# Expert values of a dense mixture, with the values as the stationary operand: 512-column matmuls become 256-column ones, and the closing transposes go

## The chip, the cores and the metric

The kernel is written in Bass and Tile for one core of a Trainium2 chip. The metric is the device time of one execution in microseconds (us). Five engines run side by side: TensorE (PE) multiplies matrices, VectorE (DVE) and ScalarE (ACT) work on vectors, GpSimd (POOL) and SyncE (SP) mostly issue transfers. A matmul multiplies a stationary operand of 128 x 128, which PE loads ahead of it (a weight load, PEld in the rows), with a moving operand of up to 512 columns, and adds into an accumulator in PSUM. PSUM has eight banks of 512 fp32 columns on each of 128 partitions.

## What is computed

The reference is one inference step of a two-layer hybrid decoder: a prompt of 256 tokens and 8 decode tokens, model width 1024. Each layer has four mixers, a cross-attention, and at the end an expert channel mixer over 16384 experts, of which every token picks 16 for each of 8 heads:

```python
act = jax.nn.gelu(jnp.einsum('td,thkd->thk', hb, u_tab[e]).astype(jnp.float32))
return jnp.einsum('thk,thkd->td', (g * act).astype(hb.dtype), v_tab[e])
...
x = x + peer_ffn(rmsnorm(x, lp['norm_ffn']), lp['peer_wq'], lp['peer_subkeys'], lp['peer_u'], lp['peer_v']).astype(x.dtype)
```

`u_tab` and `v_tab` have a row of 1024 for every expert. After the second layer a last rmsnorm gives the output.

## The kernel before

The kernel keeps the residual `x` with features in partitions: `x` is 128 partitions x 8 chunks x 264 tokens (256 prompt tokens, then 8 decode tokens), so feature f stands in chunk f // 128.

For the prompt tokens the experts are computed densely. Both tables are walked in 128 tiles of 128 experts x 1024 features (512 KB each). The first stage (`u_tile`, "u stage" below) multiplies each tile of `u_tab` with the normed tokens, 24 matmuls of 256 columns for each tile, and leaves in `HG0` and `HG1` the product of gate and gelu for every expert and token: experts of a tile in partitions, 256 tokens in columns, zero where a token has not picked the expert. The second stage ("value stage") multiplies these gates with `v_tab`. The 8 decode tokens go another way (`sample_u`, `sample_v`, `sample_out`).

Numbers are fp32, and products are made in three fp32r matmuls each: an operand is split in a high part (an ACT cast) and a low part (a DVE subtraction), and high x high, high x low and low x high are added. `load_w` does it for a weight tile (`w` is what the DMA brought, three buffers; `wh`, `wl` the parts, two buffers each), `split` for the gates (`ghl`, two buffers, tag `ga`). Every matmul is recorded at line 288, the line of the helper `mm`, so rows are told apart by the tiles that they name: `mm` for projections and the u stage, `pv` for the value stage, `var` for the sum of squares of the next rmsnorm, `tp` for transposes.

In the value stage of the kernel before the gates are stationary (128 experts x 128 tokens) and half a tile of values moves (512 features). Four accumulators `pv0` to `pv3` of 128 tokens x 512 features, one PSUM bank each, collect all 128 tiles: 2 halves of the tokens x 2 halves of the features x 3 products, 12 matmuls of 512 columns for a tile. At the end `total` takes each accumulator: ACT copies it out with the scale 1/GS (`ov`), PE transposes it in four pieces (`tp`), DVE adds them to `x`, ACT squares the sum, and PE adds the squares over the features with a matmul against a constant matrix (`var`).

The order of the instructions on each engine is set by the scheduler of the framework, save inside `tc.manual_schedule`, where PE keeps the order of the code. The tiles are loaded on SP's queue. In the middle of the value stage of the first layer (tile 62) `following()` starts the loads and small preparations of the next layer. After the value stage, in the first layer the next layer's input projection reads `x` through `eh` and `el` (scaled and split, ACT and DVE); in the second layer the last rmsnorm reads it (`yfin`, `rstd`).

Of the kernel before, what the change touches and what calls it, by code (L numbers as in the profile page):

```python
# [8 lines left out]
DEPTH, D, SEQ, DB = 2, 1024, 256, 8  # L9
NT = SEQ + DB  # L10
# [222 lines left out]
GS = 16384.0  # L233
# [10 lines left out]
def emit(tc, A, O, layers=(0, 1)):  # L244
    nc = tc.nc
    V, S, G, T = nc.vector, nc.scalar, nc.gpsimd, nc.tensor
# [8 lines left out]
    def load_consts(pool, grp):  # L255
        names = CGRP[grp]
        n = sum(coff[k][1] for k in names)
        t = pool.tile([128, n], F32, name="cst_" + grp)
        out, o, i = {}, 0, 0
        while i < len(names):  # L260
            j, s, w = i, coff[names[i]][0], 0
            while j < len(names) and coff[names[j]][0] == s + w:
                out[names[j]] = t[:, o + w:o + w + coff[names[j]][1]]
                w += coff[names[j]][1]
                j += 1
            nc.sync.dma_start(t[:, o:o + w], A['cst'][:, s:s + w])
# [20 lines left out]
    def mm(out, lhsT, rhs, start=True, stop=True, skip=False):  # L287
        T.matmul(out, lhsT, rhs, start=start, stop=stop, skip_group_check=skip)  # L288
# [8 lines left out]
    def tt(out, a, b, op, eng=None):  # L297
        (eng or V).tensor_tensor(out, a, b, op=op)  # L298
# [7 lines left out]
    def stt(out, a, s, b, op0, op1, **kw):  # L306
        V.scalar_tensor_tensor(out, a, s, b, op0=op0, op1=op1, **kw)

    def act(out, a, f, **kw):
        S.activation(out, a, f, **kw)  # L310

    def split(h, l, x):
        S.copy(h, x)  # L313
        tt(l, x, h.bitcast(F32), OP.subtract)

    x = gp.tile([128, 8, NT], F32, name="x")
    for c in range(0, 8, 2):
# [39 lines left out]
    def var(cols=NT):  # L357
        return ps([128, cols], "var", "pa")
# [109 lines left out]
    def layer(l, mx, v, following):  # L468
# [1126 lines left out]
    def peer(l, vc, xo, oo, xe, following):  # L1595
# [12 lines left out]
        fp = pe.enter_context(tc.tile_pool(name="f%d" % l, bufs=1, side="right", reuse_waits="tile"))  # L1608
# [14 lines left out]
        tp = te.enter_context(tc.tile_pool(name="t%d" % l, bufs=1, side="right", reuse_waits="tile"))  # L1623
        r = rstd(tp, v)
        hf = tp.tile([128, 8, NT], F32, name="hf", tag="sq")
        q = tp.tile([128, 16, NT], F32, name="pq")
        for c in range(16):
            if c == 4:
                rms(tp, vc('norm_ffn'), r, hf, (hh, hl))
                for j in range(2):  # L1630
                    o = ps([8, 512], "h8")
# [5 lines left out]
            o = proj(A['peer_wq'][l, c], eh if c < 8 else (hh, hl), tag="pr" if c in (2, 3, 4) else "mm")  # L1637
# [23 lines left out]
        for i in range(2):  # L1661
            s16 = tp.tile([128, 8, 2, 16], F32, name="s16")
            i16 = tp.tile([128, 8, 2, 16], U32, name="x16")
            for g4 in range(4):
                o = ps([128, 4, 128], "sc")
                for k in range(4):
                    c = g4 * 4 + k
# [7 lines left out]
            o = ps([128, 3, 128], "tp")  # L1675
# [12 lines left out]
        for c_ in range(2):  # L1688
# [17 lines left out]
        o = ps([128, 3, 8], "ex")  # L1706
# [48 lines left out]
        for t4 in range(64):  # L1755
            tsl = slice(t4 * 4, t4 * 4 + 4)
            a = fp.tile([128, 2, 2, 128, 2], F16, name="ga", bufs=2)
            b = fp.tile([128, 2, 2, 128, 2], F16, name="gb", bufs=2)
# [4 lines left out]
            o = ps([128, 4, 128], "g")  # L1763
# [5 lines left out]
            ov = o.rearrange("p t i -> p i t")  # L1769
# [8 lines left out]


        cur_tag[0] = "ps"  # L1780
        acc = [ps([128, 512], "pv%d" % i, ("pa", "pr")[i // 2]) for i in range(4)]
        nx = None
        for i2 in range(0, 128, 2):
            part = []
            for i in (i2, i2 + 1):
                vh, vl = (t.rearrange("p a b -> p (a b)") for t in load_w(A['vd'][l, i]))
                hs = HG0[:, i, :] if i < 64 else HG1[:, i - 64, :]
                ghl = fp.tile([128, 2, 256], F32R, name="ghl", tag="ga", bufs=2)
                split(ghl[:, 0], ghl[:, 1], hs)
                part.append((vh, vl, ghl[:, 0], ghl[:, 1]))  # L1790
            def terms(i, n):
                vh, vl, gh, gl = part[n]
                m, d = slice((i % 2) * 128, (i % 2) * 128 + 128), slice((i // 2) * 512, (i // 2) * 512 + 512)
                for k, (a, b) in enumerate(((gh, vh), (gh, vl), (gl, vh))):
                    mm(acc[i], a[:, m], b[:, d], start=i2 + n == 0 and k == 0, stop=i2 + n == 127 and k == 2)
            for n in range(2 if i2 < 126 else 1):
                for i in range(4):
                    terms(i, n)
            if i2 == 62:
                he.close()  # L1800
                nx = following()
            if i2 == 116:
                v = ps([128, NT], "var", "ps")
                s2 = fp.tile([128, 8, 8], F32, name="s2", tag="ua", bufs=2)
                act(s2, x[:, :, 256:264], AF.Square)
                act(warm, part[0][2][:, 0:1].bitcast(F32), AF.Sqrt, scale=0.0)
                for c in range(8):
                    mm(v[:, 256:264], cg['o1024'], s2[:, c, :], start=c == 0, stop=False, skip=True)


        def total(i):
            ov = fp.tile([128, 512], F32, name="ov", tag="gb", bufs=2)
            act(ov, acc[i], AF.Copy, scale=1.0 / GS)
            o = ps([128, 4, 128], "tp", "mm")
            for c in range(4):
                T.transpose(o[:, c, :], ov[:, c * 128:c * 128 + 128], ident)
            n = slice((i % 2) * 128, (i % 2) * 128 + 128)
            d = x[:, 4 * (i // 2):4 * (i // 2) + 4, n]
            tt(d, d, o, OP.add)
            s2 = fp.tile([128, 4, 128], F32, name="s2", tag="ga", bufs=2)  # L1820
            act(s2, d, AF.Square)
            return s2, n
        q = []
        with tc.manual_schedule(engines={mybir.EngineType.PE}):
            terms(0, 1)
            for i, nx_ in ((0, 2), (2, 1), (1, 3), (3, None)):
                if nx_ is not None:
                    terms(nx_, 1)
                q.append(total(i))
        for i, (s2, n) in enumerate(q):  # L1830
            for c in range(4):
                mm(v[:, n], cg['o1024'], s2[:, c, :], start=False, stop=i == 3 and c == 3, skip=True)
        cur_tag[0] = "pa"
        pe.close()
        return nx, v
# [9 lines left out]
    v = var()  # L1845
# [8 lines left out]
    for i, l in enumerate(layers):  # L1854
        nx, v = layer(l, nx, v, (lambda n=layers[i + 1]: Mix(n)) if i + 1 < len(layers) else last)
# [24 lines left out]
```

## Time and profile before

| | |
|---|---|
| median of 3 runs | 2437.68 us (2434.05 to 2437.69) |
| the profiled execution's own time | 2419.86 us |
| its span, first to last instruction | 2418.1 us |
| busy shares | PE 97%, PEld 88%, DVE 72%, ACT 57%, POOL 11% |
| value stage, first layer | 853.08 to 1206.05 us, 352.97 us |
| value stage, second layer | 2053.50 to 2404.72 us, 351.22 us |

The profile is one execution, 17.82 us below the median of the runs. A busy PE is not PE at its peak: a matmul's row lasts until its result is written, and rows overlap, so what a matmul costs in a stream is the spacing of the starts, and not the mean length of a row.

### The profile page before, as it was taken

What the parts mean: (1) busy time and instruction counts of PE and PEld (TensorE: products, weight loads), DVE (VectorE), ACT (ScalarE), POOL (GpSimd) and SP (SyncE); (2) the same over time, 40 slices, a digit from 0 to 9 for tenths busy, and PEclk for the clock granted to TensorE, in tenths of its full rate; (3) what the DMA queues carried; (4) which work ended last, traced back from release to release, by engine and by line L of the source; (5) the groups of instructions that cost most, each with busy time, mean ns of one, the idle gap of its engine ahead of it and who ended that gap; (6) DMA issues with size and microseconds to landing.
All of it is one profiled execution on the core that took longest, in us unless ns stands there. A gap on an engine that the chain in (4) does not pass through costs nothing.

```text
span 2418.1 us, 46703 instructions
## 1 busy us (share of the span) xinstructions
PE 2356.8 (97%) x17292; PEld 2124.1 (88%) x17292; DVE 1735.4 (72%) x3906; ACT 1380.4 (57%) x2826; POOL 264.2 (11%) x288
## 2 busy tenths in 40 slices
PE   9998999999999999999998989999999999999998
PEld 7777979999999988888887779899999999888887
DVE  6757767996698855565568577689957988555555
ACT  5544665554687745555545456655557877454444
POOL 5742000000000000000057410000000000000000
PEclk9999999999999999999999999999999999999999
DMA  8743776555675556676677338755556755566664
GB/s 284 229 109 125 274 302 203 179 175 178 203 238 182 186 189 192 193 216 193 191 228 230 99 128 312 268 196 181 177 177 214 228 190 185 183 193 194 195 192 140
DMA packets 146372, 480.63 MB, mean 199 GB/s; under 512 B 20288, under 2 KB 37728, under 8 KB 141024
## 3 DMA queue, kind: packets, MB, share of 16 engines
q1 hardware_dynamic: 129088, 423.46, 53.9%
q0 software_dynamic: 17056, 54.17, 7.5%
q8 instruction: 137, 2.24, 0.4%
q14 instruction: 91, 0.75, 0.1%
HBM read 468.53 MB, written 9.03 MB: 197 GB/s over the span
## 4 chain that ended last, share of the span: by engine, by line
PE 89%; DMA 5%; DVE 2%; ACT 2%; issue 1%; POOL 0%; SPq 0%; DVEq 0%; ACTq 0%; POOLq 0%
PE mm L288 43%; PE pv L288 28%; PE g L288 3%; DMA kvp<-in_kc 2%; PE mv L288 2%; PE asc L288 1%; PE mk L288 1%; DMA kvp<-in_vc,vidx 1%; PE xo L288 1%; PE sc L288 1%; PE xl L288 1%; PE z L288 1%; PE xm L288 1%; PE xp L288 1%; PE apv L288 1%
## 5 line engine op out<-in xcount | busy, mean ns | idle before, releaser
L313 ACT CAST wh<-w 128x1024 fp32r<-128x1024 f32 x662 | 695.6, 1051 | 745.2 <-PE pv L288 337.6
L298 DVE TENSOR_TENSOR wl<-w,wh 128x1024 fp32r<-128x1024 f32 x662 | 808.2, 1221 | 425.9 <-ACT wh L313 423.9
L288 PE MATMUL mm<-hh,wh 128*128 128x256 f32 (+1 forms) x2176 | 544.9, 287 | 1.1 <-ACT HG L310 1.1
L288 PE MATMUL mm<-hl,wh 128*128 128x256 f32 (+1 forms) x2176 | 537.3, 284 | 0.0
L288 PE MATMUL pv<-wh,ghl 128*128 128x512 f32 x2048 | 511.2, 389 | 0.5 <-ACT ghl L313 0.5
L288 PEld LDWEIGHTS pv<-wh,ghl 128*128 128x128 f32 x2048 | 384.2, 188 | 80.4 <-ACT ghl L313 0.9
L288 PEld LDWEIGHTS mm<-hl,wh 128*128 128x128 f32 x2176 | 410.1, 188 | 4.1 <-issue 4.1
L288 PEld LDWEIGHTS mm<-hh,wh 128*128 128x128 f32 x2176 | 409.9, 188 | 1.5 <-ACT HG L310 1.5
L288 PE MATMUL mm<-hh,wl 128*128 128x256 f32 (+1 forms) x2176 | 304.1, 282 | 0.0
L288 PEld LDWEIGHTS mm<-hh,wl 128*128 128x128 f32 x2176 | 279.6, 189 | 0.0
L288 PE MATMUL pv<-wl,ghl 128*128 128x512 f32 x1024 | 277.1, 389 | 0.5 <-DVE wl L298 0.5
L288 PEld LDWEIGHTS pv<-wl,ghl 128*128 128x128 f32 x1024 | 192.1, 188 | 40.6 <-DVE wl L298 1.1
L310 ACT ACTIVATE gb<-ga,ewt 128x128 f16<-128x128 f16 x512 | 173.4, 434 | 16.3 <-DVE ga L298 16.1
L1226 POOL DMA_INDIRECT kvp<-in_kc,pidx x128 | 143.2, 1119 | 233.8 <-ACT eh L310 174.5
L288 PE MATMUL mm<-eh,wh 128*128 128x264 f32 x624 | 163.7, 296 | 0.0
L288 PE MATMUL mm<-el,wh 128*128 128x264 f32 x624 | 162.0, 292 | 0.0
L288 PEld LDWEIGHTS mm<-eh,wh 128*128 128x128 f32 x624 | 119.1, 191 | 5.3 <-issue 4.1
L288 PEld LDWEIGHTS mm<-el,wh 128*128 128x128 f32 x624 | 119.4, 191 | 3.0 <-issue 2.1
L298 DVE TENSOR_TENSOR ghl<-HG,ghl 128x256 fp32r<-128x256 f32 x256 | 106.9, 418 | 0.0
L313 ACT CAST ghl<-HG 128x256 fp32r<-128x256 f32 x256 | 102.8, 402 | 2.4 <-DVE HG L298 2.4
L298 DVE TENSOR_TENSOR HG<-HG,g 128x256 f32<-128x256 f32 (+31 forms) x254 | 86.5, 348 | 17.2 <-PE g L288 16.2
L288 PE MATMUL mm<-eh,wl 128*128 128x264 f32 x624 | 94.0, 290 | 0.5 <-DVE wl L298 0.5
(675 smaller groups left out, 3214.4 us busy)
## 6 DMA issues: line engine op xcount, KB each, us to landing
w<-in_ud SPq DMA_DIRECT2D x256, 512.0 KB, 4.1
w<-in_vd SPq DMA_DIRECT2D x256, 512.0 KB, 3.5
w<-in_w_in SPq DMA_DIRECT2D x46, 512.0 KB, 5.1
kvp<-in_kc SPq DMA_DIRECT2D x128, 128.0 KB, 4.0
xkt<-in_mk SPq DMA_DIRECT2D x16, 1024.0 KB, 8.8
xkt<-in_mv SPq DMA_DIRECT2D x16, 1024.0 KB, 9.7
w<-in_peer_wq SPq DMA_DIRECT2D x32, 512.0 KB, 3.5
w<-in_x_wk SPq DMA_DIRECT2D x16, 512.0 KB, 3.6
```

The costliest lines, as they stand in the source:

```text
L288: T.matmul(out, lhsT, rhs, start=start, stop=stop, skip_group_check=skip)
L298: (eng or V).tensor_tensor(out, a, b, op=op)
L310: S.activation(out, a, f, **kw)
L313: S.copy(h, x)
L1226: nc.gpsimd.indirect_dma_start(out=t[:, j, :], out_offset=None, in_=A['kc'].rearrange("l n p f -> (l n p) f"), in_offset=bass.IndirectOffs ...
```

## The change

The two operands of the value stage change places. The values are stationary (128 experts x 128 features) and the gates move (256 tokens). The accumulators hold features in partitions, as `x` does: 8 chunks of 256 tokens, two chunks in one PSUM bank. A tile takes 8 chunks x 3 products, 24 matmuls of 256 columns. At the end there is nothing to transpose: for each chunk one DVE instruction scales the accumulator and adds it to `x`, and ACT squares it. PE keeps the code's order in the first two tiles and in the last two; in the last two it finishes chunk after chunk, both tiles for each.

```diff
-        acc = [ps([128, 512], "pv%d" % i, ("pa", "pr")[i // 2]) for i in range(4)]
+        acc = [ps([128, 2, SEQ], "pv%d" % i, ("pa", "pr")[i // 2]) for i in range(4)]
...
-            def terms(i, n):
+
+            def terms(c, n):
+
                 vh, vl, gh, gl = part[n]
-                m, d = slice((i % 2) * 128, (i % 2) * 128 + 128), slice((i // 2) * 512, (i // 2) * 512 + 512)
-                for k, (a, b) in enumerate(((gh, vh), (gh, vl), (gl, vh))):
-                    mm(acc[i], a[:, m], b[:, d], start=i2 + n == 0 and k == 0, stop=i2 + n == 127 and k == 2)
-            for n in range(2 if i2 < 126 else 1):
-                for i in range(4):
-                    terms(i, n)
+                d = slice(c * 128, c * 128 + 128)
+                for k, (a, b) in enumerate(((vh, gh), (vl, gh), (vh, gl))):
+                    mm(acc[c // 2][:, c % 2, :], a[:, d], b, start=i2 + n == 0 and k == 0 and c % 2 == 0,
+                       stop=i2 + n == 127 and k == 2, skip=True)
+            with (tc.manual_schedule(engines={mybir.EngineType.PE}) if i2 in (0, 126) else ExitStack()):
+                if i2 < 126:
+                    for n in range(2):
+                        for c in range(8):
+                            terms(c, n)
+                else:
+
+                    for c in range(8):
+                        for n in range(2):
+                            terms(c, n)
+                        d = x[:, c, 0:SEQ]
+                        stt(d, acc[c // 2][:, c % 2, :], 1.0 / GS, d, OP.mult, OP.add)
...
-        def total(i):
-            ov = fp.tile([128, 512], F32, name="ov", tag="gb", bufs=2)
-            act(ov, acc[i], AF.Copy, scale=1.0 / GS)
-            o = ps([128, 4, 128], "tp", "mm")
-            for c in range(4):
-                T.transpose(o[:, c, :], ov[:, c * 128:c * 128 + 128], ident)
-            n = slice((i % 2) * 128, (i % 2) * 128 + 128)
-            d = x[:, 4 * (i // 2):4 * (i // 2) + 4, n]
-            tt(d, d, o, OP.add)
-            s2 = fp.tile([128, 4, 128], F32, name="s2", tag="ga", bufs=2)
-            act(s2, d, AF.Square)
-            return s2, n
-        q = []
-        with tc.manual_schedule(engines={mybir.EngineType.PE}):
-            terms(0, 1)
-            for i, nx_ in ((0, 2), (2, 1), (1, 3), (3, None)):
-                if nx_ is not None:
-                    terms(nx_, 1)
-                q.append(total(i))
-        for i, (s2, n) in enumerate(q):
-            for c in range(4):
-                mm(v[:, n], cg['o1024'], s2[:, c, :], start=False, stop=i == 3 and c == 3, skip=True)
+        for c in range(8):
+            s2 = fp.tile([128, SEQ], F32, name="s2", tag="gb", bufs=2)
+            act(s2, x[:, c, 0:SEQ], AF.Square)
+            mm(v[:, 0:SEQ], cg['o1024'], s2, start=False, stop=c == 7, skip=True)
```

How the instructions stand on PE, at two places. A row gives the line, the operation, the output and the operands with the numbers of their buffers, the shape, and what the instruction waits for. First the steady part of the value stage in the second layer, one of the 128 tiles in the kernel before, all its rows:

```order
L288 MATMUL pv0_26724<-wh_29394,ghl_29398 128x512 [waits Activation_49]
L288 MATMUL pv1_26725<-wh_29394,ghl_29398 128x512
L288 MATMUL pv2_26726<-wh_29394,ghl_29398 128x512
L288 MATMUL pv3_26727<-wh_29394,ghl_29398 128x512
L288 MATMUL pv0_26724<-wl_29395,ghl_29398 128x512 [waits DVE_49]
L288 MATMUL pv1_26725<-wl_29395,ghl_29398 128x512
L288 MATMUL pv2_26726<-wl_29395,ghl_29398 128x512
L288 MATMUL pv3_26727<-wl_29395,ghl_29398 128x512
L288 MATMUL pv0_26724<-wh_29394,ghl_29398 128x512 [waits DVE_49]
L288 MATMUL pv1_26725<-wh_29394,ghl_29398 128x512
L288 MATMUL pv2_26726<-wh_29394,ghl_29398 128x512
L288 MATMUL pv3_26727<-wh_29394,ghl_29398 128x512
```

The same place in the changed kernel, 12 of a tile's 24 matmuls, from the fifth on (the four ahead of them take the first product of chunks 0, 2, 4 and 6):

```order
L288 MATMUL pv0_28239<-ghl_32371,wl_32368 128x256 [waits DVE_49]
L288 MATMUL pv1_28240<-ghl_32371,wl_32368 128x256
L288 MATMUL pv2_28241<-ghl_32371,wl_32368 128x256
L288 MATMUL pv3_28242<-ghl_32371,wl_32368 128x256
L288 MATMUL pv0_28239<-ghl_32371,wh_32367 128x256 [waits DVE_49]
L288 MATMUL pv0_28239<-ghl_32371,wh_32367 128x256
L288 MATMUL pv0_28239<-ghl_32371,wl_32368 128x256
L288 MATMUL pv0_28239<-ghl_32371,wh_32367 128x256
L288 MATMUL pv1_28240<-ghl_32371,wh_32367 128x256 x2
L288 MATMUL pv1_28240<-ghl_32371,wl_32368 128x256
L288 MATMUL pv1_28240<-ghl_32371,wh_32367 128x256
```

The waits are the same three (cast, low part of the values, low part of the gates); the matmuls are twice as many and half as wide, and no two that follow each other have the same stationary piece. The other place is the last tile of the second layer on PE. In the kernel before it is, after three matmuls of `pv0`:

```order
L288 MATMUL pv2_26726<-wh_29403,ghl_29407 128x512
L288 MATMUL pv2_26726<-wl_29404,ghl_29407 128x512
L288 MATMUL pv2_26726<-wh_29403,ghl_29407 128x512
L1816 MATMUL tp_29432<-cst_g_69,ov_29430 128x128 [waits Activation_49]
L1816 MATMUL tp_29432<-cst_g_69,ov_29430 128x128 x3
L288 MATMUL pv1_26725<-wh_29403,ghl_29407 128x512
L288 MATMUL pv1_26725<-wl_29404,ghl_29407 128x512
L288 MATMUL pv1_26725<-wh_29403,ghl_29407 128x512
L1816 MATMUL tp_29445<-cst_g_69,ov_29443 128x128 [waits Activation_49]
L1816 MATMUL tp_29445<-cst_g_69,ov_29443 128x128 x3
```

In the changed kernel the last two tiles (the operands with 32428 and 32437) begin so, with chunks 0 and 1, both in `pv0`:

```order
L288 MATMUL pv0_28239<-ghl_32428,wh_32424 128x256 [waits Activation_49]
L288 MATMUL pv0_28239<-ghl_32428,wl_32425 128x256 [waits DVE_49]
L288 MATMUL pv0_28239<-ghl_32428,wh_32424 128x256 [waits DVE_49]
L288 MATMUL pv0_28239<-ghl_32437,wh_32433 128x256 [waits Activation_49]
L288 MATMUL pv0_28239<-ghl_32437,wl_32434 128x256 [waits DVE_49]
L288 MATMUL pv0_28239<-ghl_32437,wh_32433 128x256 [waits DVE_49]
L288 MATMUL pv0_28239<-ghl_32428,wh_32424 128x256 [waits DVE_49]
L288 MATMUL pv0_28239<-ghl_32428,wl_32425 128x256
```

and go on, after chunk 2, with the squares of chunks 0 and 1 and then chunk 3:

```order
L288 MATMUL var_32146<-s2_32499,cst_g_69 128x256 [waits Activation_49]
L288 MATMUL var_32146<-s2_32502,cst_g_69 128x256 [waits Activation_49]
L288 MATMUL pv1_28240<-ghl_32428,wh_32424 128x256 [waits DVE_49]
L288 MATMUL pv1_28240<-ghl_32428,wl_32425 128x256
L288 MATMUL pv1_28240<-ghl_32428,wh_32424 128x256
```

The transposes are gone. The last tile's operands are needed from the fourth matmul of the pair on, and the first matmul of each odd chunk waits for DVE, which has to have read the even chunk out of the same bank.

## Rows read from the trace of the kernel before

**Rows 1.** The page: span, busy times, granted clock of PE in 40 slices, chain by line.

```profile
span 2418.1 us, 46703 instructions
PE 2356.8 (97%) x17292; PEld 2124.1 (88%) x17292; DVE 1735.4 (72%) x3906; ACT 1380.4 (57%) x2826; POOL 264.2 (11%) x288
...
PEclk9999999999999999999999999999999999999999
```

**Rows 2.** Busy time by stretch, value stage, second layer: stretch, length, engines, clock, DMA.

```profile
2062.00:2396.00 334.00, 334.00 (x1476) 276.54 (x1475) 191.27 (x246) 167.40 (x247) 0.00 (x0) 1.00 0.61 192
```

**Rows 3.** The chain that ended last: start, length, what, number of instructions.

```profile
585.86 5.74 PE mm L288 x48
591.60 0.07 PE g L288
...
860.30 166.06 PE pv L288 x732
...
2060.74 341.49 PE pv L288 x1506
```

**Rows 4.** The timeline of PE in the u stage: start, length, instruction, count.

```profile
835.73 0.28 PE L288 MATMUL mm<-hl,wh 128*128 128x256 f32 x1
...
837.02 1.12 PE L288 MATMUL mm<-hh,wl 128*128 128x256 f32 x8
```

**Rows 5.** The timeline at the head of the first value stage: weight loads before 8-column matmuls.

```profile
856.37 1.32 PEld L288 LDWEIGHTS var<-s,cst_g 128*128 128x128 f32 x10
```

**Rows 6.** The timeline at the end of the second value stage: how a tile is split.

```profile
2395.47 1.05 ACT L313 CAST wh<-w 128x1024 fp32r<-128x1024 f32 x1 [1.36 <-PE pv L288]
...
2396.42 0.40 ACT L313 CAST ghl<-HG 128x256 fp32r<-128x256 f32 x1
2396.56 1.23 DVE L298 TENSOR_TENSOR wl<-w,wh 128x1024 fp32r<-128x1024 f32 x1 [1.16 <-ACT wh L313]
...
2397.08 1.98 PE L288 MATMUL pv<-wh,ghl 128*128 128x512 f32 x8
2397.70 0.42 DVE L298 TENSOR_TENSOR ghl<-HG,ghl 128x256 fp32r<-128x256 f32 x1
2398.19 1.05 ACT L313 CAST wh<-w 128x1024 fp32r<-128x1024 f32 x1 [1.36 <-PE pv L288]
```

**Rows 7.** The timeline of the closing work, second layer, to the last rmsnorm.

```profile
2404.33 0.39 PE L288 MATMUL pv<-wh,ghl 128*128 128x512 f32 x1
...
2404.82 0.60 ACT L310 ACTIVATE ov<-pv 128x512 f32<-128x512 f32 x1
...
2405.89 0.60 PE L1816 MATMUL tp<-cst_g,ov 128*128 128x128 f32 x4
...
2406.99 0.68 DVE L298 TENSOR_TENSOR x<-x,tp 128x512 f32<-128x512 f32 x1
...
2407.79 0.63 ACT L310 ACTIVATE s<-x 128x512 f32<-128x512 f32 x1 [1.02 <-DVE x L298]
2408.47 1.16 PE L288 MATMUL var<-s,cst_g 128*128 128x128 f32 x8 [0.20 <-ACT s L310]
2409.67 0.48 ACT L310 ACTIVATE rstd<-var,small 128x264 f32<-128x264 f32 x1 [1.25 <-PE var L288]
```

**Rows 8.** Groups by line and shape: count, busy us, mean ns of one, idle before.

```profile
L307 DVE SCALAR_TENSOR_TENSOR xb<-sraw,pre,xb 128x256 f32<-128x256 f32 x24 | 10.3, 478 | 0.0
L310 ACT ACTIVATE x<-x 128x264 f32<-128x264 f32 x32 | 13.5, 421 | 4.3 <-DVE x L298 4.3
L288 PE MATMUL var<-x2s,cst_g 128*128 128x264 f32 x8 | 2.4, 386 | 0.0
...
L288 PEld LDWEIGHTS mm<-hh,wl 128*128 128x128 f32 x2176 | 279.6, 189 | 0.0
```

**Rows 9.** Who waited for whom, 1026 to 1040 us, first layer: total us, times, longest.

```profile
PEld pv L288 <- DVE wl L298: 1.1, 2, 0.9
PEld pv L288 <- ACT ghl L313: 0.9, 1, 0.9
```

More of the change, by code (lines that the diff above doesn't have):

```diff
@@ L1787, in peer @@
                 hs = HG0[:, i, :] if i < 64 else HG1[:, i - 64, :]
-                ghl = fp.tile([128, 2, 256], F32R, name="ghl", tag="ga", bufs=2)
+                ghl = fp.tile([128, 2, SEQ], F32R, name="ghl", tag="ga", bufs=2)
                 split(ghl[:, 0], ghl[:, 1], hs)
                 part.append((vh, vl, ghl[:, 0], ghl[:, 1]))
-            def terms(i, n):
+            def terms(c, n):
                 vh, vl, gh, gl = part[n]
-                m, d = slice((i % 2) * 128, (i % 2) * 128 + 128), slice((i // 2) * 512, (i // 2) * 512 + 512)
-                for k, (a, b) in enumerate(((gh, vh), (gh, vl), (gl, vh))):
-                    mm(acc[i], a[:, m], b[:, d], start=i2 + n == 0 and k == 0, stop=i2 + n == 127 and k == 2)
-            for n in range(2 if i2 < 126 else 1):
-                for i in range(4):
-                    terms(i, n)
+                d = slice(c * 128, c * 128 + 128)
[13 more added lines that the diff above has]
+                        stt(d, acc[c // 2][:, c % 2, :], 1.0 / GS, d, OP.mult, OP.add)
             if i2 == 62:
@@ L1803, in peer @@
                 v = ps([128, NT], "var", "ps")
-                s2 = fp.tile([128, 8, 8], F32, name="s2", tag="ua", bufs=2)
-                act(s2, x[:, :, 256:264], AF.Square)
+                s2 = fp.tile([128, 8, DB], F32, name="s2", tag="ua", bufs=2)
+                act(s2, x[:, :, SEQ:NT], AF.Square)
                 act(warm, part[0][2][:, 0:1].bitcast(F32), AF.Sqrt, scale=0.0)
                 for c in range(8):
-                    mm(v[:, 256:264], cg['o1024'], s2[:, c, :], start=c == 0, stop=False, skip=True)
-        def total(i):
-            ov = fp.tile([128, 512], F32, name="ov", tag="gb", bufs=2)
-            act(ov, acc[i], AF.Copy, scale=1.0 / GS)
-            o = ps([128, 4, 128], "tp", "mm")
-            for c in range(4):
-                T.transpose(o[:, c, :], ov[:, c * 128:c * 128 + 128], ident)
-            n = slice((i % 2) * 128, (i % 2) * 128 + 128)
-            d = x[:, 4 * (i // 2):4 * (i // 2) + 4, n]
-            tt(d, d, o, OP.add)
-            s2 = fp.tile([128, 4, 128], F32, name="s2", tag="ga", bufs=2)
-            act(s2, d, AF.Square)
-            return s2, n
-        q = []
-        with tc.manual_schedule(engines={mybir.EngineType.PE}):
-            terms(0, 1)
-            for i, nx_ in ((0, 2), (2, 1), (1, 3), (3, None)):
-                if nx_ is not None:
-                    terms(nx_, 1)
-                q.append(total(i))
-        for i, (s2, n) in enumerate(q):
-            for c in range(4):
-                mm(v[:, n], cg['o1024'], s2[:, c, :], start=False, stop=i == 3 and c == 3, skip=True)
+                    mm(v[:, SEQ:NT], cg['o1024'], s2[:, c, :], start=c == 0, stop=False, skip=True)
+        for c in range(8):
+            s2 = fp.tile([128, SEQ], F32, name="s2", tag="gb", bufs=2)
+            act(s2, x[:, c, 0:SEQ], AF.Square)
+            mm(v[:, 0:SEQ], cg['o1024'], s2, start=False, stop=c == 7, skip=True)
         cur_tag[0] = "pa"
```

## The prediction

> **What bounds the kernel now.** I read the page first [rows 1]: PE is busy for 97% of the span, at the full granted clock in all 40 slices. So a change in the number or the width of matmuls is paid or earned in full, if PE is also what the value stage waits for. The table by stretch answers that [rows 2]: in 334.00 us of the second layer's value stage PE is busy for 334.00, DVE for 191.27, ACT for 167.40, and the DMA engines for 0.61 of the time. Nothing but PE is near its limit there. The chain of waits agrees: it runs through the value stage on PE without a break, 1506 matmuls in 341.49 us and, in the first layer, 732 in 166.06 [rows 3]. That is 226.8 ns for a matmul of 512 columns. The mean of a row is longer, because rows overlap; the spacing is what counts.
>
> The change needs the price of another shape: an fp32r matmul of 256 columns with a new stationary piece each time. The u stage has just that. The chain has pieces of 48 matmuls in 5.74 us [rows 3], 119.6 ns each; between two pieces stands a small matmul of another kind, and not a wait. At 2.4 GHz, the level that the page shows, 512 columns take 213.3 ns and 256 take 106.7. So both shapes pay about the same on top, 13.5 and 12.9 ns for each matmul. This fixed part is what the change doubles.
>
> **The change part by part.**
>
> *The matmuls of the 128 tiles.* Before, 12 x 226.8 = 2.721 us for a tile; the casts of two tiles that follow each other stand 2.72 us apart (2395.47 and 2398.19, [rows 6]). After, 24 x 119.6 = 2.870 us. The difference of 0.149 us times 256 tiles in two layers is +38.1 us. Bounds: the tightest spacing in the u stage is 12 starts from 835.73 to 837.02, of which 11 gaps are 117.3 ns [rows 4]; it makes a tile 2.815 us and the term +24. The widest for this shape is the run of 8 on changing `wl` pieces, 1.12 us less one length of 0.28 over 7 gaps, 120.0 ns [rows 4]: 2.880 us and +41. If the weight load set the pace, its own spacing would count: 10 loads ahead of 8-column matmuls take 1.32 us [rows 5], less one load of 0.19 [rows 8] over 9 gaps, 126 ns; that is the first rival. I take 119.6, the mean over the long run.
>
> Here the trace and the notes part. The Trainium skill, page "TensorE: Matmul & The Clock Gate", section "Back-to-back issue gap", gives 518 cycles for 512 columns and 262 for 256 at 2.4 GHz, which is an overhead of 2.5 ns a matmul. By it a tile would go from 2.590 to 2.621 us, and the whole term would be an estimated +8 us. The rows show an overhead of 13 ns at both widths, so the sum goes by them.
>
> *What feeds PE.* Casts, subtractions and transfers for a tile stay the same in number and size, and have 0.15 us more time. One thing tightens: in the new order the low part of the values is wanted after 4 x 0.12 = 0.48 us of a tile, before after 0.91, and the low part of the gates after 0.96 instead of 1.81. Those parts become ready at a fixed time after PE has released the buffers of two tiles earlier, which is when the tile between starts. In the rows the eight matmuls at 2397.08 are four of one tile and four of the next, so a tile starts at 2397.99, and the one before at 2395.27. Then `wl` is ready at 2397.79 and the low gates at 2398.12, that is 2.52 and 2.85 us after the release [rows 6]. Wanted are they at 2.87 + 0.48 = 3.35 and 2.87 + 0.96 = 3.83. Room of 0.8 us is left, so this costs nothing; without it, each tenth of lateness would cost 26 us over the 256 tiles.
>
> *The first two tiles.* Nothing is added or taken but the order, and I count 0.
>
> *The last two tiles, second layer.* Before: from the start of the last but one tile, 2397.99, to `rstd` at 2409.67 it is 11.68 us; after the last value matmul at 2404.33 come copy, transposes, addition, square and the `var` matmuls, over 5 us [rows 7]. After, counted from the start of the pair: three matmuls run (0.36), then PE wants the last tile's operands, and by the feed above its low gates come at 2.85. So chunk 0 ends being issued at about 3.0 instead of 0.72, a loss of 2.3. Then the bank: the first matmul of chunk 1 waits until DVE has read chunk 0. That is a matmul's length 0.28, a scaled addition of 128 x 256 like the one with 478 ns [rows 8], and some 0.15 of handing over, 0.9 instead of 0.12, a loss of 0.8. Before chunks 3, 5 and 7 the `var` matmuls of two earlier chunks fill that gap; an fp32 one is two instructions each as long as a 512-column one (8 in the rows for 4 in the code, 386 ns [rows 8]), so 2 x 227 = 0.45 us. They must run anyway; beside them about 0.1 is lost each time. The pair's 48 matmuls are 5.74, six `var` 2.72, the losses 2.3 + 0.8 + 0.3: the last value matmul is issued at about 11.8. Then 0.28 of length, addition 0.48, square 0.42 [rows 8], the last `var` 0.45 and its drain, four hand-overs: `rstd` at about 13.7. That is 2.0 later than before, of which 0.3 is in the first term already: +1.7 us. So the removed transposes are paid back by waits. Bounds: without the two kinds of loss -1.7; with each gap lost in full in addition to the `var` work, +4.
>
> *The last two tiles, first layer.* The same, but behind it stands the next projection, with matmuls that can run while the squares are finished. Both weight buffers become free only with the last matmuls, before one of them a tile earlier. I take half of the second layer's term, +0.9, with bounds -2 and +4.
>
> *The middle of the first layer.* There the loads of the next layer get between the value tiles, and PE's weight loads wait for `wl` and the gates, 2.0 us in three waits [rows 9]. A slower PE asks later, by 0.15 us for each of some four tiles: I take -0.6, bounds -2 and 0.
>
> **Sum.** 38.1 + 1.7 + 0.9 - 0.6 = +40.1 us, so 2419.86 + 40.1 = 2460.0 for an execution like the profiled one, and a span of 2458. The median of the runs lies 17.8 us above that execution; PE's work is the same in each, so I add the same 40 to it: 2437.7 + 40.1 = 2477.8 us, 1.6% slower.
>
> **The rivals.**
>
> *The weight load sets the pace.* For: PE has one load for each matmul, loads are busy for 88% of the span [rows 1], and one lasts longer (0.19, [rows 8]) than the new spacing. The change doubles them. Against: the u stage doubles them just so and keeps 119.6. If each costs 126 ns, a tile takes 3.02 us and the total is +77, so 2517.
>
> *The time goes by columns alone.* Then a matmul of 256 costs half of one of 512, 113.4 ns, the tiles cost the same, and only the ends are left: +2 us, 2440, no change that can be told. Against it: no long run in the u stage has so small a spacing; the smallest is 117.3 [rows 4]. The formula quoted above from the Trainium skill ("TensorE: Matmul & The Clock Gate") lands near this rival, with its +8.
>
> *Faster.* If the 13 ns were not paid for a 256-column matmul at all, because the load of the next piece and the writing of the last result hide behind the columns, a tile would take 24 x 106.7 = 2.560 us, and the total is -0.16 x 256 = -41 plus the ends, 2399. It decides below 113.4 ns a matmul, less 2/6144 us for the ends. Against it stands every row of the u stage, with the same operands' types and the same load for each matmul.
>
> *The feed becomes late.* If the room of 0.8 us is used up, by a transfer that lands later or by a release that the new order makes later, every tile waits; 0.15 us each would give another +38, 2516. Against: the room above, and transfers busy for 0.61 of the time, of which a slower stage leaves more free.
>
> **How the numbers follow.** Less than 0.2% (4.9 us) can hardly be told from no change. Forecast (115 to 122 ns a matmul) 0.86; weight load 0.04; columns alone 0.04; faster 0.02; late feed 0.04. The range takes the forecast's bounds: low +24 with ends of -2, so 2459.7, and since an execution like the profiled one would read 2460, 2457; high +41 with ends of +8, 2487, and up to 2496 for a part of a late feed. Slower 0.94, same 0.04, faster 0.02.
>
> **What would show it.** In the changed profile the value stage should show about 3072 matmuls of 256 columns a layer, 24 in 2.87 us, so some 367 us of PE without a break, casts 2.87 us apart, PE still busy for all of it. The pair at the end should show PE idle for about 2 us before the fourth matmul, waiting for DVE's low gates, and again before chunk 1. Casts 3.0 us apart with PE always busy would be the weight load; 2.72 the columns; PE idle in each tile the feed. The prediction is wrong if the spacing of these matmuls is not that of the u stage.

## The result, and the profile after

The changed kernel takes 2478.84 us in the median of four runs (2472.16 to 2489.85), and the ratio to the kernel before is 1.0179, with a 95% interval of 1.016 to 1.0198. That is 1.8% slower; the medians differ by 41.2 us. 2477.8 was predicted. The profiled execution is the longest of the four, 2489.85 us with a span of 2488.1, while the one before was 18 us below its median. So the two pages are not subtracted from each other; the value stages are compared by themselves.

First the page of the changed kernel, the rows that answer to [rows 1]:

```profile
span 2488.1 us, 52712 instructions
...
PE 2407.7 (97%) x20300; PEld 2288.4 (92%) x20300; DVE 1735.8 (70%) x3914; ACT 1379.6 (55%) x2826; POOL 261.9 (11%) x288
...
PEclk9899999999999999999999999999999999999999
```

Some 3,000 matmuls more, and 50 us more of PE. Where they are, the table by stretch says, second value stage without its ends (answers to [rows 2]), and then the chain that ended last (answers to [rows 3]; start, length, what, number of instructions):

```profile
2111.00:2460.00 349.00, 349.00 (x2911) 349.00 (x2910) 188.82 (x242) 165.78 (x245) 0.00 (x0) 1.00 0.60 183
```

```profile
601.01 5.74 PE mm L288 x48
...
877.99 170.03 PE pv L288 x1416
...
1063.75 169.71 PE pv L288 x1412
...
2110.71 354.35 PE pv L288 x2952
```

PE does not wait for anything in 349 us. 354.35 us over 2952 matmuls are 120.0 ns from start to start, where the kernel before needed 226.8 for twice the columns. The u stage, which the change does not touch, still has its 5.74 us for 48. New in the table is the second pair of numbers: the weight loads are busy for 349.00 of 349.00 us, before for 276.54 of 334. A load's row is 0.19 us long and the loads now start 0.12 apart, so this alone does not show that they set the pace.

The casts of ACT show what that makes of a tile, and the end of the second layer (timeline of ACT; in brackets the idle time before, and what ended it):

```profile
2462.20 1.05 ACT L313 CAST wh<-w 128x1024 fp32r<-128x1024 f32 x1 [1.52 <-PE pv L288]
...
2465.08 1.05 ACT L313 CAST wh<-w 128x1024 fp32r<-128x1024 f32 x1 [1.52 <-PE pv L288]
...
2479.67 0.48 ACT L310 ACTIVATE rstd<-var,small 128x264 f32<-128x264 f32 x1 [0.79 <-PE var L288]
```

2.88 us from tile to tile, before 2.72 [rows 6]. From the cast of the last tile (2465.08) to `rstd` it is 14.59 us; before it was 2409.67 less 2398.19, 11.48 [rows 6, 7]. PE's own timeline shows what fills them:

```profile
2465.12 0.28 PE L288 MATMUL pv<-ghl,wh 128*128 128x256 f32 x1
2466.49 0.39 PE L288 MATMUL pv<-ghl,wh 128*128 128x256 f32 x1 [1.09 <-ACT ghl L313]
2467.44 0.38 PE L288 MATMUL pv<-ghl,wl 128*128 128x256 f32 x1 [0.57 <-DVE wl L298]
2467.78 0.38 PE L288 MATMUL pv<-ghl,wh 128*128 128x256 f32 x1
2468.68 0.58 PE L288 MATMUL pv<-ghl,wh 128*128 128x256 f32 x1 [0.52 <-DVE x L307]
2469.06 0.41 PE L288 MATMUL pv<-ghl,wl 128*128 128x256 f32 x1
2469.27 0.63 PE L288 MATMUL pv<-ghl,wh 128*128 128x256 f32 x2
2469.70 0.41 PE L288 MATMUL pv<-ghl,wl 128*128 128x256 f32 x1
```

Three matmuls of the last tile stand alone (the second to fourth row), each behind an operand that comes late, and the fifth row is chunk 1 behind DVE's reading of the bank. After that nothing is late any more, and yet the starts stand 0.21 us apart (three in 0.64 between 2469.06 and 2469.70) instead of 0.12. The table by stretch gives the reason, the granted clock in the last column but two:

```profile
2465.00:2467.40 2.40, 0.79 (x5) 0.38 (x3) 1.24 (x2) 1.35 (x2) 0.00 (x0) 1.00 0.00 0
2468.70:2471.20 2.50, 2.50 (x12) 2.50 (x13) 1.10 (x3) 0.76 (x2) 0.00 (x0) 0.50 0.00 0
2472.00:2478.00 6.00, 6.00 (x42) 5.39 (x41) 3.38 (x10) 2.09 (x5) 0.00 (x0) 1.00 0.00 0
1237.30:1240.00 2.70, 2.70 (x12) 2.70 (x13) 0.92 (x2) 1.36 (x4) 0.00 (x0) 0.50 0.43 168
```

After 2.4 us in which PE was busy for 0.79 the granted clock is 0.50, that is 1.2 GHz, for the 12 matmuls of chunks 1 and 2, and at 2472 it is back at 1.00, 2.4 GHz. The last row is the same place in the first layer; there it is 0.50 from 1235.90 to 1242.70.

### The profile page after: what moved, and what is told of

Read it like the earlier page. It is cut to its first block, busy times and chain, and to the rows that moved or that the text cites. A ratio compares the mean times of both kernels' runs of the same rounds, so it can differ in the third digit from the quotient of the medians.

```text
span 2488.1 us, 52712 instructions
## 1 busy us (share of the span) xinstructions
PE 2407.7 (97%) x20300; PEld 2288.4 (92%) x20300; DVE 1735.8 (70%) x3914; ACT 1379.6 (55%) x2826; POOL 261.9 (11%) x288
## 4 chain that ended last, share of the span: by engine, by line
PE 86%; DMA 5%; DVE 3%; ACT 2%; issue 2%; POOL 1%; SPq 0%; another core or an unknown queue 0%; DVEq 0%; POOLq 0%; ACTq 0%
PE mm L288 40%; PE pv L288 29%; PE g L288 3%; DMA kvp<-in_kc 2%; PE mv L288 2%; PE asc L288 1%; PE mk L288 1%; DVE wl L298 1%; PE xo L288 1%; PE xl L288 1%; DMA w<-in_peer_wq 1%; PE ob L288 1%; PE sc L288 1%; DMA kvp<-in_vc,vidx 1%; PE z L288 1%
## 5 line engine op out<-in xcount | busy, mean ns | idle before, releaser
L288 PE MATMUL pv<-ghl,wh 128*128 128x256 f32 x4096 | 666.5, 284 | 3.2 <-ACT ghl L313 2.2
L288 PEld LDWEIGHTS pv<-ghl,wh 128*128 128x128 f32 x4096 | 589.0, 193 | 4.9 <-ACT ghl L313 2.6
L288 PE MATMUL pv<-ghl,wl 128*128 128x256 f32 x2048 | 460.9, 284 | 1.8 <-DVE wl L298 1.8
L288 PEld LDWEIGHTS pv<-ghl,wl 128*128 128x128 f32 x2048 | 341.3, 193 | 2.6 <-DVE wl L298 2.6
```

## The experiments

What was to be told apart: is it the number of matmuls that costs, at a fixed price each, or the exchange of the operands and the new ending; and what is the price made of, the weight load or something else? Experiments with cut columns or features change how much is computed; their chain of waits is read, and not their time. One execution of a kernel lies up to 0.7% from another, so only the timed ones are given a ratio. The kernel before ran on the same chip each time; it took 2419 to 2433 us there, less than the 2437.7 of the first comparison, so the times that were expected are read as differences.

**Splitting alone.** The kernel before, with each product cut in two:

```diff
-                    mm(acc[i], a[:, m], b[:, d], start=i2 + n == 0 and k == 0, stop=i2 + n == 127 and k == 2)
+                    for e in range(2):
+                        f = slice(d.start + 256 * e, d.start + 256 * e + 256)
+                        mm(acc[i][:, 256 * e:256 * e + 256], a[:, m], b[:, f], start=i2 + n == 0 and k == 0 and e == 0,
+                           stop=i2 + n == 127 and k == 2, skip=True)
```

> The kernel before, with its gates stationary and its own ending, but each value product of 512 columns is made as two of 256 that follow each other on one stationary piece: 24 matmuls a tile instead of 12, nothing else. If each matmul has a fixed price beside its columns: spacing 119.6 to 120 ns, a tile 2.87 to 2.88 us, +38 to +41 us on 2437.7, so 2476 to 2479 (ratio 1.016 to 1.017). If the price lies in the exchange of the operands, in the order or in the new ending: 2438 to 2443. If a repeated piece is cheaper than a new one, between the two.

Measured: 2456.38 us beside 2420.39 for the kernel before, ratio 1.0151 [1.0127, 1.0174]. Its chain, second value stage:

```profile
2077.44 360.57 PE pv L288 x3004
```

That is 120.0 ns, the changed kernel's number, with the old operands' places and the old ending. So the number of matmuls makes the matmuls' loss by itself: 40.8 us by the spacing, 36.0 in the medians, with an interval of 30.7 to 42.1. Who is stationary is no part of the spacing. In the code each stationary piece is used twice in a row; the trace does not show whether the scheduler kept that in the steady part. In the last tile, where PE keeps the code's order, the second use of a piece starts 117 to 120 ns after the first, save behind transposes; so there is no sign that a piece that was just loaded is loaded cheaper.

**Fewer columns.** The changed kernel with 192, then 128 of the 256 tokens moving:

```diff
-                    mm(acc[c // 2][:, c % 2, :], a[:, d], b, start=i2 + n == 0 and k == 0 and c % 2 == 0,
+                    mm(acc[c // 2][:, c % 2, 0:192], a[:, d], b[:, 0:192], start=i2 + n == 0 and k == 0 and c % 2 == 0,
...
-                        d = x[:, c, 0:SEQ]
-                        stt(d, acc[c // 2][:, c % 2, :], 1.0 / GS, d, OP.mult, OP.add)
+                        d = x[:, c, 0:192]
+                        stt(d, acc[c // 2][:, c % 2, 0:192], 1.0 / GS, d, OP.mult, OP.add)
```

> The changed kernel, but only 192 of the 256 tokens move in the value stage, so the last 64 prompt tokens get no expert values. The number of matmuls and of weight loads stays. Fixed price beside the columns: 80.0 + 13 = 93 ns from start to start in the second value stage, about 2.24 us a tile and some 160 us less in all. Weight load as the pace: the spacing stays at 120 ns and the time at about 2479.

> The changed kernel, but only 128 of the 256 tokens move in the value stage, so the other 128 prompt tokens get no expert values. With 192 columns the spacing was 111.7 ns, neither 93 nor 120. If a weight load sets a floor below the columns' own price: 111 to 112 ns again. If load and columns partly add, a line through 120.0 at 256 and 111.7 at 192 goes on: 103 ns. Columns and 13 ns alone: 67 ns.

The chains, 192 columns in the second layer, then 128 columns in the first and the second:

```profile
2060.23 329.74 PE pv L288 x2952
```

```profile
871.88 155.51 PE pv L288 x1392
...
1042.61 311.74 PE pv L288 x1460
...
2231.03 629.87 PE pv L288 x2952
```

With 192 columns it is 111.7 ns: both numbers that were expected are wrong. With 128 it is 111.7 again while the clock is at 2.4 GHz (155.51 us over 1392). So below some width the spacing does not follow the columns any more; there is a floor of 111.7 ns. It is not a wait for operands: from 2100 to 2300 us of the kernel with 192 columns ACT's casts wait 99.5 us for PE. From 1042.61 on and in the second layer the kernel with 128 columns ran at another clock, and that is told at the end.

**A shorter load.** The changed kernel with 64 of each 128 features as the stationary piece, with 192 and with all 256 columns:

```diff
-                d = slice(c * 128, c * 128 + 128)
+                d = slice(c * 128, c * 128 + 64)
...
-                    mm(acc[c // 2][:, c % 2, :], a[:, d], b, start=i2 + n == 0 and k == 0 and c % 2 == 0,
+                    mm(acc[c // 2][0:64, c % 2, 0:256], a[:, d], b[:, 0:256], start=i2 + n == 0 and k == 0 and c % 2 == 0,
```

> The changed kernel with 192 of the 256 tokens moving and with 64 of each 128 features as the stationary piece, so half of the features and a quarter of the tokens get no expert values: a shorter load at the same count. If the load of 128 features made the floor of 111.7 ns: 93 ns, columns and 13. If the floor has another cause, such as the issue of an instruction: 111 to 112 ns again.

> The changed kernel with all 256 tokens moving, but with 64 of each 128 features as the stationary piece, so half of the features get no expert values. If the 120.0 ns of the changed kernel are columns and a fixed price: 120 ns again. If the length of the load is a part of them: 110 to 116 ns, and the changed kernel is partly bound by its loads after all.

With 192 columns the tiles come faster than their operands, so that PE waits (for `w`, `wl` and `ghl`); a piece of its timeline without a wait:

```profile
2097.70 0.25 PE L288 MATMUL pv<-ghl,wl 128*64 128x192 f32 x1
2097.79 0.42 PE L288 MATMUL pv<-ghl,wh 128*64 128x192 f32 x3
2098.05 0.25 PE L288 MATMUL pv<-ghl,wl 128*64 128x192 f32 x1
2098.14 0.43 PE L288 MATMUL pv<-ghl,wh 128*64 128x192 f32 x3
2098.41 0.25 PE L288 MATMUL pv<-ghl,wl 128*64 128x192 f32 x1
2098.50 0.42 PE L288 MATMUL pv<-ghl,wh 128*64 128x192 f32 x3
2098.76 0.25 PE L288 MATMUL pv<-ghl,wl 128*64 128x192 f32 x1
```

From 2097.70 to 2098.76 there are 12 gaps of 88 ns each, no floor of 111.7 any more: that floor was made by the stationary piece of 128. It is also 5 ns less than the 93 that columns and 13 ns would take. The chain with 256 columns, second layer:

```profile
2077.96 336.89 PE pv L288 x2972
```

113.4 ns instead of 120.0. That is what neither the prediction nor its rival of columns and a constant price had: a stationary piece of half the width takes 6.6 ns off a matmul whose columns are the same.

**The same at full width.** Is it the load that is shorter, or the output that is narrower? In the kernel before a load of 128 hides behind 512 columns, so halving it can only show the output:

```diff
-                m, d = slice((i % 2) * 128, (i % 2) * 128 + 128), slice((i // 2) * 512, (i // 2) * 512 + 512)
+                m, d = slice((i % 2) * 128, (i % 2) * 128 + 64), slice((i // 2) * 512, (i // 2) * 512 + 512)
...
-                    mm(acc[i], a[:, m], b[:, d], start=i2 + n == 0 and k == 0, stop=i2 + n == 127 and k == 2)
+                    mm(acc[i][0:64], a[:, m], b[:, d], start=i2 + n == 0 and k == 0, stop=i2 + n == 127 and k == 2)
```

> A control on the kernel before, all of its 512 columns moving: 64 of each 128 tokens as the stationary piece, so half of the prompt tokens get no expert values. With 256 columns halving the stationary piece took the spacing from 120.0 to 113.4 ns. If that was the shorter load, it cannot show here, where the load hides behind twice the columns: 226.8 ns again. If it was the narrower output or array: about 213 to 220 ns.

```profile
2067.28 346.43 PE pv L288 x1506
```

230.0 ns, 3 more than with the full piece, which neither theory expected. So a narrower output does not make a matmul cheaper by itself, and that speaks for the load as what gained at 256 columns; why it costs 3 ns here stays open.

**Widths between.** The kernel before with 320 and with 384 of each 512 features moving, the product low x low added so that PE has enough to do:

```diff
-                m, d = slice((i % 2) * 128, (i % 2) * 128 + 128), slice((i // 2) * 512, (i // 2) * 512 + 512)
-                for k, (a, b) in enumerate(((gh, vh), (gh, vl), (gl, vh))):
+                m, d = slice((i % 2) * 128, (i % 2) * 128 + 128), slice((i // 2) * 512, (i // 2) * 512 + 320)
+                for k, (a, b) in enumerate(((gh, vh), (gh, vl), (gl, vh), (gl, vl), (gl, vl))):
```

> The kernel before with 320 of each 512 features moving, so 3 of 8 features get no expert values, and with the product low x low added twice, 20 matmuls a tile, so that the operands come in time. The full load of 128 is as long as some 250 columns and should be hidden. If a matmul has a fixed price of 13.3 ns beside its columns at any width: 133.3 + 13.3 = 146.7 ns. If the price goes with the columns, 226.8 for 512 and 113.4 for 256 with a short load, and only the load adds at 256: 141.8 ns.

> The same with 384 of each 512 features moving, a quarter of the features without expert values, and the product low x low added once, 16 matmuls a tile. Fixed price at any width: 160.0 + 13.3 = 173.3 ns. A price that goes with the columns: 170.1 ns.

The chains, second layer, 320 columns and 384:

```profile
2086.26 367.64 PE pv L288 x2506
```

```profile
2066.76 348.16 PE pv L288 x2008
```

146.7 and 173.4 ns: the fixed price, to a tenth. With 256 and 512 columns there are now four widths, with a new piece of 128 for each matmul, and beside the columns at 2.4 GHz each has 13.3 to 13.5 ns on top (120.0 - 106.7, 146.7 - 133.3, 173.4 - 160.0, 226.8 - 213.3). That the price goes with the columns is out.

**Two pieces to an operand.** In the joined matmuls further below, operands of 512 columns in two separate pieces seemed dearer than those in one. (The 242 ns in the expectation are misread: the trace of that run has eight of them from 611.48 to 613.34, 233 ns each.) The kernel before, with such operands in the value stage:

```diff
-                    mm(acc[i], a[:, m], b[:, d], start=i2 + n == 0 and k == 0, stop=i2 + n == 127 and k == 2)
+                    b = b.rearrange("p (a h q) -> p a h q", a=2, h=2)[:, :, i // 2, :]
+                    mm(acc[i].rearrange("p (a q) -> p a q", a=2), a[:, m], b, start=i2 + n == 0 and k == 0, stop=i2 + n == 127 and k == 2)
```

> The kernel before, but each moving operand of 512 columns is two pieces of 256 that do not lie side by side (features 0 to 255 with 512 to 767, and the rest), all else alike. In the u stage with joined matmuls such operands of two pieces stood 242 ns apart and not 227. If the fixed price belongs to a piece and not to a matmul: 240 to 243 ns here, and about 47 us more in all. If it belongs to the matmul: 226.8 ns and the time of the kernel before.

2429.34 us in one execution, beside 2432.9; the chain is that of the kernel before to the hundredth, 226.8 ns:

```profile
2070.22 341.49 PE pv L288 x1506
```

So the price belongs to a matmul, not to a piece of its operand. Why those of the joined matmuls stand 233 ns apart stays open.

**Another order at the end.** The changed kernel with the last tile behind the last but one, and even chunks ahead of odd ones:

```diff
                     for c in range(8):
-                        for n in range(2):
-                            terms(c, n)
+                        terms(c, 0)
+                    for c in (0, 2, 4, 6, 1, 3, 5, 7):
+                        terms(c, 1)
                         d = x[:, c, 0:SEQ]
```

> The changed kernel with another order in the last two tiles: all chunks of the last but one tile, then the last tile's chunks in the order 0, 2, 4, 6, 1, 3, 5, 7, each followed by its addition. If the waits in the closing pair are what it costs beside the matmuls: no idle PE for the last tile's operands, the clock stays at full, from the start of the pair to rstd in the second layer about 9 us instead of 14.8, and with 2 to 4 us in the first layer 8 to 10 us less than the changed kernel, 2469 to 2471. If the eight additions on DVE and the next layer's first transfers set those ends anyway: 0 to 3 us less.

2455.34 us beside 2420.39, ratio 1.0145 [1.0121, 1.017]. The interval overlaps that of the changed kernel a little, so the time alone does not prove a gain; the place does. ACT's timeline at the end of the second layer, and the stretch in which the changed kernel had waited:

```profile
2435.50 1.05 ACT L313 CAST wh<-w 128x1024 fp32r<-128x1024 f32 x1 [1.53 <-PE pv L288]
...
2442.29 0.85 ACT L310 ACTIVATE s<-x 128x256 f32<-128x256 f32 x2 [0.48 <-PE var L288]
...
2445.91 0.48 ACT L310 ACTIVATE rstd<-var,small 128x264 f32<-128x264 f32 x1 [0.79 <-PE var L288]
```

```profile
2438.00:2442.00 4.00, 4.00 (x31) 3.80 (x31) 3.40 (x12) 1.14 (x3) 0.00 (x0) 1.00 0.00 0
```

From the cast to `rstd` it is 10.41 us instead of 14.59; from 2438 to 2442 us PE is never idle, and the clock stays at 1.00. Expected were some 5.8 less (9 for 14.8); 4.2 came, because the squares, with two buffers, now wait for the `var` matmuls (0.48 in the second row), and those for the squares. From the first value matmul to `rstd` the two layers together take 756.6 us, the changed kernel 764.3.

**Wider matmuls in the u stage.** If a matmul's fixed price is what counts, the opposite step should earn it. Kernel before, high u times both parts of the tokens at once:

```diff
+        hx = fp.tile([128, 8, 2, NT], F32R, name="hx")
+        hh, hl = hx[:, :, 0], hx[:, :, 1]
...
-            o = proj(A['ud'][l, i2], (hh[:, :, 0:256], hl[:, :, 0:256]), 256)
+            wh, wl = load_w(A['ud'][l, i2])
+            oo = ps([128, 2, 256], "mm", "mm")
+            for c in range(8):
+                mm(oo, wh[:, c, :], hx[:, c, :, 0:256], start=c == 0, stop=False, skip=True)
+            for c in range(8):
+                mm(oo[:, 0], wl[:, c, :], hx[:, c, 0, 0:256], start=False, stop=c == 7, skip=True)
+            o = fp.tile([128, 256], F32, name="uo", bufs=2)
+            S.copy(o, oo[:, 1])
+            tt(o, o, oo[:, 0], OP.add)
```

> The opposite step in the u stage of the kernel before: high u times high and low tokens as one matmul of 512 columns into two halves of a bank, low u times high tokens of 256 columns as ever; ACT copies one half out and DVE adds the other. 8 matmuls of 512 and 8 of 256 a tile instead of 24 of 256. Fixed price a matmul: 8 x 0.2268 + 8 x 0.1196 = 2.771 instead of 2.870 us, -25 us over 256 tiles, 2412 (ratio 0.990). Rival: the copy and the addition, some 0.9 us a tile on ACT and DVE, which are up to 83% busy in the u stage, make PE wait: 2430 to 2450. Time by columns alone: 2438 or more.

2449.98 us beside 2420.39, ratio 1.0124 [1.0102, 1.0145]: slower, as the rival had it, and by more. Its 2430 to 2450 mean at most 12 us more; measured are 29.6. Where nothing else is between, PE does get shorter, from 5.74 us for two tiles to

```profile
600.41 43.83 PE mm L288 x248
```

15.5 tiles in 43.83 us, 2.83 each for 2.87. But PE now waits for the sum, from 248 to 600 us (who waited for whom: total, times, longest):

```profile
PEld mm L288 <- DVE uo L298: 11.8, 19, 1.6
PE mm L288 <- DVE uo L298: 7.6, 13, 1.4
```

Then the same for the first 64 tiles only, the sum made by ACT and POOL:

```diff
+            if i2 < 64:
...
+                ob = fp.tile([128, 2, 256], F32, name="uo", bufs=2)
+                o = ob[:, 0]
+                S.copy(ob, oo)
+                tt(o, o, ob[:, 1], OP.add, eng=G)
```

> The kernel before with the joined matmuls (512 columns for high u) only in the first 64 tiles of the u stage, and the sum of the halves taken off DVE: ACT copies both halves out, POOL adds them. If a load that hides behind 512 columns is worth what the value stage lost, a tile is 0.08 to 0.1 us shorter where PE sets the pace: 10 to 13 us less over both layers, ratio 0.995. If the longer way from matmul to gelu or the port that POOL and DVE share makes PE wait: no change or slower by up to 15 us, as with the addition on DVE.

2422.98 us beside 2419.35, ratio 1.0019 [1.0006, 1.0033]: no gain, rather a small loss. ACT's gelu now waits for POOL, 29.7 us in 30 waits from 248 to 600:

```profile
ACT HG L310 <- POOL uo L298: 29.7, 30, 1.7
```

That these waits ate the whole gain is likely, and not shown. No version here beats the kernel before.

## Why the prediction was right, step by step

**The matmuls.** The term was 256 tiles x 0.149 us = 38.1, from the u stage's 119.6 ns. Measured are 120.0, the upper bound: 2.880 less 2.721 us is 0.159 a tile, +40.8. The step that "both shapes pay about the same on top" and that the change doubles this part holds: splitting alone gives it, and four widths show 13.3 to 13.5 ns.

**What the fixed part is** the prediction left open, and it is no constant of the instruction. With a stationary piece of 64 it is 6.7 ns at 256 columns, 8 at 192 and 16.7 at 512 (230.0 - 213.3). At 113.4 ns a tile of 24 matmuls takes 2.722 us, what a tile took before, but with pieces of 64 it does half of the products, so this is no way out. A load that merely sticks out behind the columns does not explain the fixed part: it would be hidden at 512 columns, and there the 13.5 ns are the same with a piece of 128. What the fixed part is made of stays open.

**The rival that the weight load sets the pace** was closer than its chance of 0.04. There is a floor, 111.7 ns and not 126; the 126 came from 8-column matmuls of another type [rows 5]. The u stage was taken as evidence against it, but its rows pay for the same load. The floor does not bind at 256 columns, since 106.7 + 13.3 is more; by the two numbers it would below some (111.7 - 13.3) x 2.4 = 236 columns, an estimate. The Trainium skill ("TensorE: Matmul & The Clock Gate", section "LDWEIGHTS (loading the stationary operand)") has 1/1.2 ns for each stationary column, 107 ns for 128; the floor in the traces at 2.4 GHz, 111.7, is 5 ns above that. **Columns alone** is out: 120.0 and not 113.4. With it goes the +8 that the prediction worked out from the Trainium skill.

**Feed.** Right: PE busy 349.00 of 349.00 us. **First two tiles**: at the head of the stage nothing waited. **Middle**: -0.6 was counted, since PE would ask later; PE's weight loads wait 1.0 us in two waits there, before 2.0 in three [rows 9]; PE's matmuls 0.6, before 1.0.

**The last two tiles, second layer.** Predicted as waits of 2.3 us for the last tile's operands and 0.8 for the bank, +1.7 in all. Both are there, in the order that was said: the third matmul of that tile is issued at 2467.78, 2.9 us after the pair's start (0.2 ahead of the cast at 2465.08), and chunk 1 0.9 later. It is no single wait of 2 us for DVE, as its signs had it, but 1.1 for ACT's cast of the gates, 0.6 for `wl` and the rest for the low gates. But `rstd` comes 3.1 later than before, not 2.0: the term left out the clock, 12 matmuls at 213 instead of 120 ns, 1.1 us. With the other order nothing stalls, the clock stays at 1.00, and `rstd` comes 1.1 us earlier than in the kernel before (10.41 for 11.48).

**The last two tiles, first layer.** +0.9 was too small. ACT's rows at that place in the kernel before; the cast at 1199.40 is that of the last tile, with its gates behind it:

```profile
1199.40 1.05 ACT L313 CAST wh<-w 128x1024 fp32r<-128x1024 f32 x1 [1.36 <-PE pv L288]
1200.36 0.40 ACT L313 CAST ghl<-HG 128x256 fp32r<-128x256 f32 x1
...
1213.44 0.48 ACT L310 ACTIVATE rstd<-var,small 128x264 f32<-128x264 f32 x1 [0.79 <-PE var L288]
```

And in the changed kernel:

```profile
1233.48 1.05 ACT L313 CAST wh<-w 128x1024 fp32r<-128x1024 f32 x1 [1.52 <-PE pv L288]
...
1252.30 0.48 ACT L310 ACTIVATE rstd<-var,small 128x264 f32<-128x264 f32 x1 [2.50 <-PE var L288]
```

That is 18.8 us from the last tile's cast to the next layer's `rstd`, before 14.0: 4.8 later. The other order brings it to 15.3. PE has projections to do in that time, so not all of it need lengthen the run.

**The sum.** The median lies 1 us from the predicted 2477.8, and that is partly luck. The ratio's 1.0179 on 2437.68 is +43.6, with an interval of +39.0 to +48.3. In the profiled executions, from the first value matmul to the `rstd` behind the stage, in us:

| | first layer | second layer | both, beside before |
|---|---|---|---|
| before | 360.6 | 356.4 | |
| changed | 384.8 | 379.5 | +47.3 |
| each product split | 379.7 | 376.6 | +39.3 |
| changed, other order at the end | 381.3 | 375.3 | +39.6 |

These are single executions, but the stretch repeats well: the run with POOL's sum, whose value stage is the old one, has 360.5 and 356.4. Of the 47.3 us 40.8 are the matmuls, so some 6.5 are left for the two ends with the middle, where the prediction had 2.0. The other order takes 7.7 us off, and its 39.6 leave nothing for the ends beside the 40.8. So the step that carries the forecast was right and its term was 2.7 too small; the terms of the ends were too small by 4.5 together.

## What to carry to other kernels

Price a matmul by the spacing of long runs at its own width and type, and count matmuls as well as columns: here a new stationary piece of 128 cost 13.3 ns beside the columns from 256 to 512, so an exchange of operands that halves the moving side pays it twice. Before saving transposes at an end of some 10 us, multiply the price by the number of tiles, and look at what the new order of the ending makes late. A row that shows the new shape already is the best price, but it doesn't tell what the price is made of, and a rival is not excluded by a row that carries its cost too.

## What was not expected of the hardware

- After a stall of 2.4 us with PE busy for 0.79 in the second layer, and the same waits in the first, the granted clock fell to 0.50, 1.2 GHz, for some 3 us in the second layer and 6.8 in the first. With the other order at the end there was no such stall, and the clock stayed at 1.00 at both places. At 0.50 256 columns stood 213 ns apart, which is 256 / 1.2: nothing on top. It is no shorter with a stationary piece of 64 (10 gaps of 213 ns from 2418.68 to 2420.81), so the load is not what sets it there. The Trainium skill ("TensorE: Matmul & The Clock Gate", section "Back-to-back issue gap") has N / 1.2 at this level, and the trace agrees; for 2.4 GHz it has 2.5 ns on top, where these rows have 13.3.
- With 128 columns PE and its loads were busy without a gap, and still the clock was at 0.50, in the first layer behind the waits in the middle of the stage, in the second almost from its start, where PE had been busy for 6.60 of 6.60 us from 2218.00 to 2224.60 before it fell. The spacing at 0.50 was 213.4 ns (629.87 us over 2952), 1.9 times the 111.7 at 1.00, so the floor goes with the clock. With 192 columns it is 213 at 0.50 as well (10 gaps from 1200.28 to 1202.41). That kernel took 2886.28 us in its one execution, with fewer columns than any other. The table by stretch for this kernel, then the stretch with 192 columns and the one with pieces of 64:

```profile
900.00:1000.00 100.00, 100.00 (x898) 100.00 (x897) 58.59 (x75) 50.22 (x75) 0.00 (x0) 1.00 0.63 198
2300.00:2800.00 500.00, 500.00 (x2346) 500.00 (x2346) 151.71 (x196) 131.55 (x195) 0.00 (x0) 0.50 0.34 103
```

```profile
1199.96:1202.60 2.64, 2.64 (x12) 2.64 (x13) 0.85 (x2) 1.42 (x4) 0.00 (x0) 0.50 0.49 174
```

```profile
2418.41:2420.90 2.49, 2.49 (x12) 2.49 (x13) 1.11 (x3) 0.81 (x2) 0.00 (x0) 0.50 0.00 0
```

- A stationary piece of half the width made a matmul cheaper at 256 columns (120.0 to 113.4 ns) and dearer at 512 (226.8 to 230.0).
